# Early up blocks of a decoder block on one core: the second product is added to the first one's copy at once, and the row factors keep the order of the source

## The chip, the cores and the metric

One Trainium2 chip, one core. The metric is device time in microseconds (us), the median of several executions; lower is better. The profile is of one execution on the same core. Engines: TensorE (PE in the profile) for matmuls, VectorE (DVE), ScalarE (ACT), GpSimd (POOL), and the queue of SyncE (SP), which issues most transfers.

## The reference, cut to what matters

A decoder block: an RWKV-7 mixer beside sliding-window attention, both merged by gates, and then a gated feed-forward with a short convolution. All of it is float32, 512 rows, model width 2048, feed-forward width 5632. The change lies at the seam between the output projection and the feed-forward:

```python
x = x + (g_rw * p_rw + g_att * p_att) @ w_out[l]
x = x + conv_ffn(rms_norm(x, norm2_g[l]), w_up[l], conv_w[l], conv_b[l], w_down[l])

def conv_ffn(h, w_up, conv_w, conv_b, w_down):
    u = h @ w_up
    up = jnp.pad(u, ((0, 0), (CONV_W - 1, 0), (0, 0)))
    c = up[:, 0:S] * conv_w[0] + up[:, 1:S + 1] * conv_w[1] + up[:, 2:S + 2] * conv_w[2] + conv_b
    val, gate = jnp.split(c, 2, axis=-1)
    return (jax.nn.silu(gate) * val) @ w_down
```

## The kernel before, in words

Every large product runs in three matmuls of a reduced float32 form: each operand is split into a high part and a low part, and high·high, high·low and low·high are summed in PSUM. ScalarE makes the high part by a copy (`whi`, L1090, or L1055 for a row factor) and VectorE the low part by a subtraction (`wlo`, L1091, or L1056).

The three projections `w_out`, `w_up` and `w_down` are each done as 2x2 blocks with seven products instead of eight. For `w_up` the rows of the normalised input `h` are split into two halves and its 2048 channels into two halves; that gives four quarters: `q11`, `q12`, `q21`, `q22` (in the lists of instructions the tiles `x_13090`, `x_13091`, `x_13092`, `x_13093`). From them come seven **row factors**, each split into high and low once: `b11`, `b21`, `b22` are quarters themselves, and `t3 = q22 - q12`, `t1 = q11 - q12`, `t2 = -t1 - q22`, `t4 = -t2 - q21` are made in place in the quarters (tiles 128x2048). In the lists the pairs high/low are `t_15898`/`t_15899` for t1, `t_15900`/`t_15901` for t3, `t_15902`/`t_15903` for t2, `t_15904`/`t_15905` for t4 and `b_15896`/`b_15897` for b22.

The 5632 feed-forward columns go by in 44 **blocks** `f` of 128, value and gate together. Each block has seven **steps** P1, P2, P7, P6, P5, Q4, P3, each of 24 matmuls 128x256 (eight slices of channels by three matmuls). P1 and P2 are summed, the others go into a chain of sums. P1, P6, P5 and P3 of a block all write the same half of a PSUM bank (`X`), one after the other, so each waits until the one before has been taken out by ScalarE (L1124). In blocks 0 to 3 the sum of P2 goes to the other half of that same bank (`Z`).

A table `steps` sets the order: P1 of blocks 0 to 3, then P2 of blocks 0 to 3, then P7 of blocks 0 to 3; from there, for blocks 0 and 1, P6(0), P5(0), P6(1), P3(0), P5(1), Q4(0), P3(1), Q4(1), the same for blocks 2 and 3, and from block 4 on one block at a time. The first four blocks thus start on factors that exist early, while the rest of the row factors are being made. `run(i)` prepares step i+2 (`prep`: for P6 and P3 a sum of two weight tiles on VectorE, L1084, then `whi` and `wlo`), issues the matmuls of step i, and takes its result out (`Block.out`). From step 12 on, `prep` also issues up to two pieces of the convolution of earlier blocks. `whi` and `wlo` live in rings of three buffers, so the `whi` of a step waits for the matmuls of the step three before it.

The quarters `q12` and `q22` reach TensorE last: `transposed` multiplies them by a diagonal of the norm factors into PSUM (eight tiles of 128x256 in `ps_t`, L1039), and each is evicted with a scale, the even ones on ScalarE (L1048), the odd ones on VectorE (L1046).

Instructions of an engine run in the order in which they stand in its list. `pin` (`tc.keep_in_program_order`) keeps an instruction in the order of the source among all those that carry it; one without it is placed by a scheduler. In the kernel before, the evictions, the four passes that make t3, t1, t2, t4 and the splits of the row factors carry none.

In blocks 0 to 3, P1 is copied by ScalarE to a tile `t1` of its own (L1117, not the row factor), and the sum of P2 stays in PSUM until the tiles `u` of the convolution exist; then VectorE writes `u = t1 + Z` (L1128). This is done for blocks 0 and 1 ahead of step 12, P6(0), for block 2 behind P6(2), and for block 3 behind Q4(2).

Of the kernel before, what the change touches and what calls it, by code (L numbers as in the profile page):

```python
# [8 lines left out]
F32 = mybir.dt.float32  # L9
# [3 lines left out]
AF = mybir.ActivationFunctionType  # L13
ALU = mybir.AluOpType
# [120 lines left out]
def block_kernel(ctx: ExitStack, tc: tile.TileContext, d: Dims, a: dict, out: bass.AP):  # L135
# [723 lines left out]
    TH = S // 2  # L859
# [170 lines left out]
    def transposed(tps, i, q, dg=None):  # L1030

        pss = []
        for k in range(KH):
            if k % 2 == 0:
                pss.append(tps.tile([P, 2, TH], F32, name="ps_t", tag="tp"))
            for t in range(NT // 2):
                dst, src = pss[-1][:, k % 2, t * P : (t + 1) * P], q[:, t, k * P : (k + 1) * P]
                if dg:
                    pe.matmul(dst, src, dg[t], start=True, stop=True)  # L1039
                else:  # L1040
                    pe.transpose(dst, src, ident)
        for k in range(KH):
            src, g = pss[k // 2][:, k % 2], col("n2g", i * KH + k)
            dst = q[:, 2 * k // KH, k % (KH // 2) * TH : (k % (KH // 2) + 1) * TH]
            if k % 2:
                dve.tensor_scalar(dst, src, g, None, op0=ALU.mult)  # L1046
            else:
                act.activation(dst, src, AF.Copy, scale=g)  # L1048

    def halves(t):  # L1050
        return t.rearrange("p (a k) s -> p a (k s)", a=2)

    def split_q(n, q):
        hi, lo = (halves(x) for x in bq[n])
        act.activation(hi, q, AF.Copy)  # L1055
        dve.tensor_tensor(lo, q, hi.bitcast(F32), op=ALU.subtract)  # L1056

    us = []
    dve.tensor_scalar(cw[:, 0:3, NF:], cw[:, 0:3, NF:], -1.0, None, op0=ALU.mult)
# [4 lines left out]
    class Block:  # L1064
# [46 lines left out]
        def out(self, n):  # L1111
            X, Y, Z = self.X, getattr(self, "Y", None), self.Z
            if n == "P7":
                return
            if n == "P1" and self.f < NPRE:
                self.t1 = up.tile([P, TH], F32, name="t1", tag="t1", bufs=NPRE)
                pin(act.activation(self.t1, X, AF.Copy))  # L1117
                return

            i, j, ps, first = {"P1": (0, 0, X, True), "P2": (0, 0, Z, False), "P6": (1, 0, X, True), "P5": (1, 1, X, True),  # L1120
                               "Q4": (1, 0, Y, False), "P3": (0, 1, X, True)}[n]
            u = us[self.f % 2][:, i, 2 + j * TH : 2 + (j + 1) * TH]
            if first:
                pin(act.activation(u, ps, AF.Copy))  # L1124
                if n == "P5":
                    pin(dve.tensor_tensor(u, u, Y, op=ALU.add))
            else:
                pin(dve.tensor_tensor(u, self.t1 if n == "P2" and self.f < NPRE else u, ps, op=ALU.add))  # L1128

        def conv(self, part):  # L1130

# [75 lines left out]
    def run(i):  # L1207
        f, n = steps[i]
        prep(i + 2, 2 if 3 * NPRE <= i < 7 * NPRE else 1)
        B[f].mm(n)  # L1210
        if n != "P2" or f >= NPRE:
            B[f].out(n)
        if n == "P3":
            if f % 2 == 0:
                wp["add"] = sums_along()
# [45 lines left out]
    run(2)  # L1261
    transposed(tps, 0, q12, dg)
    run(3)
    dve.tensor_tensor(q11, q11, q12, op=ALU.subtract)
    transposed(tps, 1, q22, dg)
    tpx.close()
    run(4)
    dve.tensor_tensor(q12, q22, q12, op=ALU.subtract)
    split_q("t3", q12)
    tcx.close()  # L1270
    x1q.close()
# [3 lines left out]
    run(7)  # L1275
    upy = psx.enter_context(tc.tile_pool(name="uppy", bufs=4, space=PSUM, side="right", reuse_waits="tile"))
    run(8)
    dve.scalar_tensor_tensor(q11, q11, -1.0, q22, op0=ALU.mult, op1=ALU.subtract)
    split_q("t2", q11)
    run(9)  # L1280
    run(10)
    split_q("b22", q22)
    run(11)
    dve.scalar_tensor_tensor(q21, q11, -1.0, q21, op0=ALU.mult, op1=ALU.subtract)
    split_q("t4", q21)
    x1s.close()
    upu = upx.enter_context(tc.tile_pool(name="upu", bufs=1, side="left", reuse_waits="tile"))
# [5 lines left out]
    upc = upcx.enter_context(tc.tile_pool(name="upc", bufs=1, side="right", reuse_waits="tile"))  # L1293
    hp0 = upcx.enter_context(tc.tile_pool(name="hhl0", bufs=1, side="right", reuse_waits="tile"))
    for f in range(2):
        B[f].out("P2")
    for i in range(3 * NPRE, len(steps)):
        run(i)
        if steps[i] in ((2, "P6"), (2, "Q4")):
            B[2 + (steps[i][1] == "Q4")].out("P2")  # L1300
        if steps[i] == (NF - 2, "P7"):
            first_h = fetch("dn", 0, 0, hp0, pin)
        if steps[i] == (NF - 1, "P7"):
# [103 lines left out]
```

## Time and profile before

| | |
|---|---|
| device time, median of 3 runs | 2952.3 us (2951.39 to 2952.68) |
| profiled execution, first to last instruction | 2946.4 us |
| that span and the median differ by | 5.9 us |
| TensorE busy | 2897.7 us |
| VectorE busy | 1949.0 us |
| ScalarE busy | 1316.0 us |

The profiled execution gives the span, not the device time; the 5.9 us lie around the span. Times below are counted from the start of the span. "Idle before" is the time an engine stood still ahead of an instruction, with what ended it.

### The profile page before, as it was taken

To read this page: it belongs to the slowest core of one execution; us is meant where nothing else is said; L and a number is where in the kernel's file an instruction comes from. 1 tells how busy PE (TensorE), PEld (TensorE's weight loads), DVE (VectorE), ACT (ScalarE), POOL (GpSimd) and SP (SyncE) were. 2 spreads that over 40 slices of the span, in tenths; PEclk is the share of its full clock that TensorE was granted. 3 is DMA by queue.
4 is the path that set the end of the run, shared out by engine and by line. 5 is a ranking of instruction groups with operands and counts; after the bars stand their busy time and mean duration, and the time that the engine had idled before them with its cause. 6 is when DMAs were issued, how large, how long until landed. Compare 5 with 4: busy or idle time off the path is not lost.

```text
span 2946.4 us, 48467 instructions
## 1 busy us (share of the span) xinstructions
PE 2897.7 (98%) x18922; PEld 2473.2 (84%) x18922; DVE 1949.0 (66%) x3242; ACT 1316.0 (45%) x2134; POOL 219.4 (7%) x286
## 2 busy tenths in 40 slices
PE   7999999999999999999999899999999999999999
PEld 6777777777777777688888899999999999888887
DVE  5555666666666666344567877778777778665555
ACT  4344434434334334232346554554554555544444
POOL 0001000000000000101000011011011011000000
PEclk9999999999999999999999999999999999999999
DMA  6855656656656656878877788888888888877775
GB/s 185 210 151 153 178 139 154 159 129 161 158 131 162 155 129 170 250 223 262 275 243 247 193 242 236 230 227 225 234 239 235 227 229 237 311 240 242 256 258 189
DMA packets 225142, 609.47 MB, mean 207 GB/s; under 512 B 24768, under 2 KB 44944, under 8 KB 223888
## 3 DMA queue, kind: packets, MB, share of 16 engines
q1 hardware_dynamic: 157504, 434.92, 45.9%
q0 software_dynamic: 36064, 132.14, 23.3%
q10 hardware_dynamic: 31344, 39.31, 3.9%
q8 instruction: 148, 2.42, 0.3%
q14 instruction: 82, 0.67, 0.1%
HBM read 556.62 MB, written 174.43 MB: 248 GB/s over the span
## 4 chain that ended last, share of the span: by engine, by line
PE 92%; DVE 3%; ACT 2%; DMA 2%; issue 1%; ACTq 0%; SPq 0%; DVEq 0%
PE X L1108 17%; PE X L975 11%; PE acc L262 10%; PE acc L261 10%; PE acc L260 10%; PE Y L975 8%; PE Y L1108 8%; PE Z L1108 4%; PE psG L758 1%; PE bulk L689 1%; PE mi L505 1%; PE bulk L751 1%; PE psS L769 1%; PE bulk L728 1%; DMA raw<-in_w_z_dram 1%
## 5 line engine op out<-in xcount | busy, mean ns | idle before, releaser
L262 PE MATMUL acc<-xhi,wlo 128*128 128x512 f32 x1120 | 460.0, 411 | 0.7 <-DVE wlo L244 0.7
L260 PE MATMUL acc<-xhi,whi 128*128 128x512 f32 x1120 | 454.9, 406 | 4.0 <-ACT whi L243 4.0
L261 PE MATMUL acc<-xlo,whi 128*128 128x512 f32 x1120 | 453.9, 405 | 0.0
L243 ACT ACTIVATE whi<-raw 128x512 fp32r<-128x512 f32 x352 | 220.0, 629 | 491.3 <-PE acc L261 326.2
L968 DVE TENSOR_TENSOR wlo<-raw,whi 128x1024 fp32r<-128x1024 f32 x210 | 257.0, 1224 | 203.4 <-ACT whi L967 202.4
L244 DVE TENSOR_TENSOR wlo<-raw,whi 128x512 fp32r<-128x512 f32 x352 | 240.3, 688 | 205.1 <-ACT whi L243 198.1
L967 ACT ACTIVATE whi<-raw 128x1024 fp32r<-128x1024 f32 x210 | 222.6, 1060 | 289.3 <-PE X L975 151.8
L1108 PE MATMUL X<-b,whi 128*128 128x256 f32 x1472 | 270.4, 284 | 2.3 <-DVE u L1128 0.9
L1108 PE MATMUL X<-t,whi 128*128 128x256 f32 x1408 | 258.9, 284 | 8.7 <-DVE u L1128 8.3
L1091 DVE TENSOR_TENSOR wlo<-raw,whi 128x1024 fp32r<-128x1024 f32 x176 | 215.1, 1223 | 77.5 <-ACT whi L1090 77.2
L1108 PE MATMUL Y<-t,whi 128*128 128x256 f32 x1408 | 257.1, 283 | 0.0
L262 PEld LDWEIGHTS acc<-xhi,wlo 128*128 128x128 f32 x1120 | 211.3, 189 | 44.2 <-issue 3.1
L260 PEld LDWEIGHTS acc<-xhi,whi 128*128 128x128 f32 x1120 | 211.6, 189 | 43.2 <-ACT whi L243 5.2
L261 PEld LDWEIGHTS acc<-xlo,whi 128*128 128x128 f32 x1120 | 211.3, 189 | 40.3 <-issue 3.1
L1090 ACT ACTIVATE whi<-a 128x1024 fp32r<-128x1024 f32 x132 | 139.3, 1056 | 216.4 <-DVE a L1084 213.2
L1108 PEld LDWEIGHTS X<-b,whi 128*128 128x128 f32 x1472 | 230.7, 193 | 3.1 <-issue 2.4
L1108 PEld LDWEIGHTS X<-t,whi 128*128 128x128 f32 x1408 | 220.8, 193 | 9.3 <-DVE u L1128 5.7
L1108 PEld LDWEIGHTS Y<-t,whi 128*128 128x128 f32 x1408 | 219.6, 192 | 0.0
L1108 PE MATMUL X<-b,wlo 128*128 128x256 f32 x736 | 209.1, 284 | 2.1 <-DVE wlo L1091 2.1
L1091 DVE TENSOR_TENSOR wlo<-a,whi 128x1024 fp32r<-128x1024 f32 x132 | 161.7, 1226 | 68.2 <-ACT whi L1090 67.6
L1108 PE MATMUL X<-t,wlo 128*128 128x256 f32 x704 | 200.1, 284 | 0.1
L1108 PE MATMUL Y<-t,wlo 128*128 128x256 f32 x704 | 199.2, 283 | 0.0
(346 smaller groups left out, 6151.2 us busy)
## 6 DMA issues: line engine op xcount, KB each, us to landing
raw<-in_w_up_dram SPq DMA_DIRECT2D x180, 512.0 KB
raw<-in_w_z_dram SPq DMA_DIRECT2D x288, 256.0 KB
s_dn<-in_w_dn_dram POOLq DMA_DIRECT2D x88, 512.0 KB, 6.3
raw<-in_w_up_dram POOLq DMA_DIRECT2D x88, 512.0 KB, 8.7
raw<-s_dn SPq DMA_DIRECT2D x88, 512.0 KB
raw<-in_w_dn_dram SPq DMA_DIRECT2D x66, 512.0 KB
a<-in_w_up_dram SPq DMA_DIRECT2D x48, 512.0 KB
s_dn<-in_w_dn_dram SPq DMA_DIRECT2D x44, 512.0 KB
```

The source lines that it names most:

```text
L243: pin(act.activation(hi, raw, AF.Copy))
L244: pin(dve.tensor_tensor(lo, raw, hi.bitcast(F32), op=ALU.subtract))
L260: pe.matmul(acc, whi[:, j], xhi[:, k], start=first, stop=False)
L261: pe.matmul(acc, whi[:, j], xlo[:, k], start=False, stop=False)
L262: pe.matmul(acc, wlo[:, j], xhi[:, k], start=False, stop=last)
L505: pe.matmul(ps[:, h], pT[:, kb, h], vt[:, n - 1 + kb, g * HD : (g + 1) * HD], start=kb == kbs[0], stop=kb == kbs[-1])
L967: act.activation(whi, wr, AF.Copy)
L968: dve.tensor_tensor(wlo, wr, whi.bitcast(F32), op=ALU.subtract)
L975: pe.matmul(dst, l[:, q, ts], r[:, es], start=fst and j == 0, stop=lst and j == 2, skip_group_check=True)
L1090: pin(act.activation(hi, t, AF.Copy))
L1091: pin(dve.tensor_tensor(lo, t, hi.bitcast(F32), op=ALU.subtract))
L1108: pin(pe.matmul(ps, l[:, k], r[:, k], start=start and k + i == 0, stop=last and i == 2, skip_group_check=True))
```

## The change

It has four parts. The sum of P2 of blocks 0 to 3 is added to the copy `t1` as soon as P2 is done (VectorE, in place), and ScalarE copies `t1` to `u` where VectorE added before (`begin`). The evictions, the four passes and the splits of the row factors are pinned. In the two batches that use the diagonal, six of eight evictions go to ScalarE and two to VectorE, instead of four and four. And two lines of the source change places: the split of t2 stands behind `run(9)`, the pass that makes t1 behind the second batch.

```diff
-            if k % 2:
-                dve.tensor_scalar(dst, src, g, None, op0=ALU.mult)
+            if k % (4 if dg else 2) == 1:
+                pin(dve.tensor_scalar(dst, src, g, None, op0=ALU.mult))
             else:
-                act.activation(dst, src, AF.Copy, scale=g)
+                pin(act.activation(dst, src, AF.Copy, scale=g))
...
-        act.activation(hi, q, AF.Copy)
-        dve.tensor_tensor(lo, q, hi.bitcast(F32), op=ALU.subtract)
+        pin(act.activation(hi, q, AF.Copy))
+        pin(dve.tensor_tensor(lo, q, hi.bitcast(F32), op=ALU.subtract))
...
+            if n == "P2" and self.f < NPRE:
+                pin(dve.tensor_tensor(self.t1, self.t1, Z, op=ALU.add))
+                return
...
+        def begin(self):
+            pin(act.activation(us[self.f % 2][:, 0, 2 : 2 + TH], self.t1, AF.Copy))
...
     run(3)
-    dve.tensor_tensor(q11, q11, q12, op=ALU.subtract)
     transposed(tps, 1, q22, dg)
     tpx.close()
+    pin(dve.tensor_tensor(q11, q11, q12, op=ALU.subtract))
     run(4)
-    dve.tensor_tensor(q12, q22, q12, op=ALU.subtract)
+    pin(dve.tensor_tensor(q12, q22, q12, op=ALU.subtract))
...
-    dve.scalar_tensor_tensor(q11, q11, -1.0, q22, op0=ALU.mult, op1=ALU.subtract)
+    pin(dve.scalar_tensor_tensor(q11, q11, -1.0, q22, op0=ALU.mult, op1=ALU.subtract))
+    run(9)
     split_q("t2", q11)
-    run(9)
...
-    dve.scalar_tensor_tensor(q21, q11, -1.0, q21, op0=ALU.mult, op1=ALU.subtract)
+    pin(dve.scalar_tensor_tensor(q21, q11, -1.0, q21, op0=ALU.mult, op1=ALU.subtract))
...
     for f in range(2):
-        B[f].out("P2")
+        B[f].begin()
...
         if steps[i] in ((2, "P6"), (2, "Q4")):
-            B[2 + (steps[i][1] == "Q4")].out("P2")
+            B[2 + (steps[i][1] == "Q4")].begin()
```

Since the change moves instructions, three places of the order follow. First VectorE around the two batches of the diagonal, from the `wlo` of P2(0) on; before:

```order
L1091 TENSOR_TENSOR wlo<-raw,whi 128x1024
L1046 TENSOR_SCALAR x_13091<-ps_t,par 128x256 x4
L1264 TENSOR_TENSOR x_13090<-x_13090,x_13091 128x2048
L1091 TENSOR_TENSOR wlo<-raw,whi 128x1024
L1056 TENSOR_TENSOR t_15899<-x_13090,t_15898 128x2048
L1046 TENSOR_SCALAR x_13093<-ps_t,par 128x256 x4
L1091 TENSOR_TENSOR wlo<-raw,whi 128x1024
L1268 TENSOR_TENSOR x_13091<-x_13093,x_13091 128x2048
L1278 SCALAR_TENSOR_TENSOR x_13090<-x_13090,x_13093 128x2048
L1056 TENSOR_TENSOR t_15901<-x_13091,t_15900 128x2048
```

and now, from the evictions of the second batch on (L1116 is the new addition, on the tiles `t1` of blocks 0 to 3):

```order
L1046 TENSOR_SCALAR x_13093<-ps_t,par 128x256 x2
L1271 TENSOR_TENSOR x_13090<-x_13090,x_13091 128x2048
L1091 TENSOR_TENSOR wlo<-raw,whi 128x1024
L1116 TENSOR_TENSOR t_15941<-t_15941,X 128x256
L1273 TENSOR_TENSOR x_13091<-x_13093,x_13091 128x2048
L1056 TENSOR_TENSOR t_15901<-x_13091,t_15900 128x2048
L1091 TENSOR_TENSOR wlo<-raw,whi 128x1024
L1116 TENSOR_TENSOR t_15994<-t_15994,X 128x256
L1091 TENSOR_TENSOR wlo<-raw,whi 128x1024
L1116 TENSOR_TENSOR t_16028<-t_16028,X 128x256
L1056 TENSOR_TENSOR t_15899<-x_13090,t_15898 128x2048
L1091 TENSOR_TENSOR wlo<-raw,whi 128x1024
```

The pass for t1 (L1264, now L1271) and its low part have moved behind the second batch, the low part of t3 now comes ahead of that of t1, and the pass for t2 (L1278) has left this place. Second, VectorE up to the weight sum of P6(1); before (`a` tiles are weight sums, L1084: `a_16065` for block 0, then `a_16196`, now named `a_16198`, for block 1):

```order
L1084 TENSOR_TENSOR a_16065<-a_16065,raw 128x1024
L1284 SCALAR_TENSOR_TENSOR x_13092<-x_13090,x_13092 128x2048
L1091 TENSOR_TENSOR wlo<-a_16065,whi 128x1024
L1091 TENSOR_TENSOR wlo<-raw,whi 128x1024
L1056 TENSOR_TENSOR t_15905<-x_13092,t_15904 128x2048
L1128 TENSOR_TENSOR u_16391<-t_15941,X 128x256
L1128 TENSOR_TENSOR u_16393<-t_15994,X 128x256
L1084 TENSOR_TENSOR a_16196<-a_16196,raw 128x1024
```

and now:

```order
L1283 SCALAR_TENSOR_TENSOR x_13090<-x_13090,x_13093 128x2048
L1091 TENSOR_TENSOR wlo<-raw,whi 128x1024
L1056 TENSOR_TENSOR t_15903<-x_13090,t_15902 128x2048
L1084 TENSOR_TENSOR a_16065<-a_16065,raw 128x1024
L1091 TENSOR_TENSOR wlo<-a_16065,whi 128x1024
L1056 TENSOR_TENSOR b_15897<-x_13093,b_15896 128x2048
L1091 TENSOR_TENSOR wlo<-raw,whi 128x1024
L1289 SCALAR_TENSOR_TENSOR x_13092<-x_13090,x_13092 128x2048
L1056 TENSOR_TENSOR t_15905<-x_13092,t_15904 128x2048
L1084 TENSOR_TENSOR a_16198<-a_16198,raw 128x1024
```

The pass for t2 (L1283) and the low parts of t2 and b22, which stood further up before, now stand between the weights of P7(2) and the weight sum of P6(1), and the two additions to `u` are gone. Third, ScalarE at the same place; before:

```order
L1055 ACTIVATE t_15902<-x_13090 128x2048
L1090 ACTIVATE whi<-raw 128x1024 x2
L1090 ACTIVATE whi<-a_16065 128x1024
L1090 ACTIVATE whi<-raw 128x1024
L1055 ACTIVATE t_15904<-x_13092 128x2048
L1090 ACTIVATE whi<-a_16196 128x1024
L1124 ACTIVATE u_16391<-X 128x256
```

and now:

```order
L1055 ACTIVATE t_15902<-x_13090 128x2048
L1090 ACTIVATE whi<-a_16065 128x1024
L1055 ACTIVATE b_15896<-x_13093 128x2048
L1090 ACTIVATE whi<-raw 128x1024
L1055 ACTIVATE t_15904<-x_13092 128x2048
L1134 ACTIVATE u_16395<-t_15941 128x256
L1134 ACTIVATE u_16397<-t_15994 128x256
L1090 ACTIVATE whi<-a_16198 128x1024
L1127 ACTIVATE u_16395<-X 128x256
```

The high part of t2 now comes behind the `whi` of P7(2) and P7(3), that of b22 (before further up) behind the `whi` of P6(0), and the copies `begin` (L1134) stand ahead of the `whi` of P6(1). The last row, here L1127, before L1124, is in both lists the instruction that takes P6(0) out of `X`. The lists of TensorE, GpSimd and of the SP queue keep their order.

More of the change, by code (lines that the diff above doesn't have):

```diff
@@ L1127, in out @@
             else:
-                pin(dve.tensor_tensor(u, self.t1 if n == "P2" and self.f < NPRE else u, ps, op=ALU.add))
+                pin(dve.tensor_tensor(u, u, ps, op=ALU.add))
+        def begin(self):
+            pin(act.activation(us[self.f % 2][:, 0, 2 : 2 + TH], self.t1, AF.Copy))
         def conv(self, part):
@@ L1210, in run @@
         B[f].mm(n)
-        if n != "P2" or f >= NPRE:
-            B[f].out(n)
+        B[f].out(n)
         if n == "P3":
```

## The prediction

> **What bounds the kernel now.** I read the page first, then busy time by stage, then what TensorE waited for in the stage of the change, then the places of those waits.
>
> ```profile
> span 2946.4 us, 48467 instructions
> PE 2897.7 (98%) x18922; PEld 2473.2 (84%) x18922; DVE 1949.0 (66%) x3242; ACT 1316.0 (45%) x2134; POOL 219.4 (7%) x286
> ```
>
> TensorE is busy for 98% of the span. A change that leaves its work alone can only move the remaining idle time, or the clock. The stretches (TensorE busy, then weight loads, VectorE, ScalarE, GpSimd, granted clock, transfers) say where it lies:
>
> ```profile
> 1610.00:1715.04 105.04, 92.42 (x738) 91.28 (x739) 83.38 (x101) 56.41 (x75) 10.49 (x14) 0.95 0.80 222
> 1715.04:2521.00 805.96, 805.82 (x6713) 805.41 (x6713) 636.50 (x764) 413.66 (x562) 83.88 (x97) 1.00 0.86 231
> 2521.00:2946.40 425.40, 420.37 (x1857) 347.49 (x1856) 254.33 (x267) 202.14 (x231) 2.14 (x4) 1.00 0.74 251
> ```
>
> From 1715 us on TensorE hardly stops (0.14 us idle in 806), so a shift at 1715 reaches the end undiminished. Before it, in the first four blocks, 12.6 us are idle and the clock averages 0.95. There, by what ended each wait (us in total, times, longest):
>
> ```profile
> PE X L1108 <- DVE u L1128: 9.2, 3, 5.5
> PE X L1108 <- DVE wlo L1091: 2.1, 1, 2.1
> PE X L1108 <- DVE x L989: 0.9, 1, 0.9
> PE X L1108 <- ACT u L1124: 0.5, 1, 0.5
> PE X L1108 <- ACT whi L1090: 0.5, 1, 0.5
> ```
>
> Most of it is L1128, the late addition that the change takes away. The places, with the last matmul batch of the diagonal (start, length, instruction, idle before):
>
> ```profile
> 1625.49 3.73 PE L1039 MATMUL ps_t<-dg,x 128*128 128x128 f32 x32
> 1638.32 0.51 PE L1108 MATMUL X<-b,whi 128*128 128x256 f32 x2 [0.47 <-ACT whi L1090]
> 1640.97 0.58 PE L1108 MATMUL X<-b,wlo 128*128 128x256 f32 x1 [2.14 <-DVE wlo L1091]
> 1659.57 0.48 PE L1108 MATMUL X<-t,whi 128*128 128x256 f32 x2 [2.76 <-DVE u L1128]
> 1663.14 0.50 PE L1108 MATMUL X<-t,whi 128*128 128x256 f32 x2 [0.47 <-ACT u L1124]
> 1691.94 0.80 PE L1108 MATMUL X<-t,whi 128*128 128x256 f32 x2 [5.51 <-DVE u L1128]
> 1709.06 0.48 PE L1108 MATMUL X<-b,whi 128*128 128x256 f32 x2 [0.94 <-DVE u L1128]
> ```
>
> By the table of steps these are P2(3) (two rows), P6(0), P5(0), P5(2) and P3(3). A wait has an after-effect on the clock (column behind the count, windows chosen around the waits), and with it on the steps that follow (start, length, matmuls):
>
> ```profile
> 1641.00:1644.40 3.40, 3.40 (x16) 0.52 0.90 265
> 1692.00:1695.40 3.40, 3.40 (x16) 0.50 1.03 181
> 1695.40:1705.00 9.60, 9.60 (x82) 1.00 0.82 240
> 1656.80:1659.60 2.80, 0.04 (x2) 1.00 0.66 184
> ```
>
> ```profile
> 1663.14 11.77 PE X L1108 x96
> 1691.94 13.31 PE X L1108 x96
> 1712.16 2.88 PE Y L1108 x24
> ```
>
> A step takes 2.88 us, so 96 matmuls take 11.52. Behind the wait of 5.51 they took 13.31: 3.4 us at half clock, 1.79 us lost. Behind the waits at P6(0) and P5(0) the clock stayed at 1.00, and 0.25 us was lost.
>
> **The change, part by part.** What the removed addition frees is bounded by what is late next. Durations of the other pieces (mean ns behind the bar's busy time), then single rows of both engines around P6(0), P5(0) and P5(2):
>
> ```profile
> L1091 DVE TENSOR_TENSOR wlo<-raw,whi 128x1024 fp32r<-128x1024 f32 x16 | 19.4, 1222 | 4.1 <-ACT whi L1090 4.1
> L1090 ACT ACTIVATE whi<-raw 128x1024 fp32r<-128x1024 f32 x16 | 16.6, 1050 | 5.8 <-PE X L1108 3.2 <-PE Y L1108 2.5
> L1084 DVE TENSOR_TENSOR a<-a,raw 128x1024 f32<-128x1024 f32 x8 | 9.7, 1219 | 0.0
> L1056 DVE TENSOR_TENSOR t<-x,t 128x2048 fp32r<-128x2048 f32 x4 | 9.2, 2290 | 1.2 <-ACT t L1055 1.2
> L1055 ACT ACTIVATE t<-x 128x2048 fp32r<-128x2048 f32 x4 | 7.6, 1908 | 1.6 <-DVE x L1268 1.4
> L1048 ACT ACTIVATE x<-ps_t,par 128x256 f32<-128x256 f32 x8 | 3.5, 470 | 2.0 <-PE ps_t L1039 1.6 <-ACT x L1048 0.3
> ```
>
> ```profile
> 1649.65 1.22 DVE L1091 TENSOR_TENSOR wlo<-raw,whi 128x1024 fp32r<-128x1024 f32 x1
> 1650.79 1.22 DVE L1084 TENSOR_TENSOR a<-a,raw 128x1024 f32<-128x1024 f32 x1
> 1651.92 2.28 DVE L1284 SCALAR_TENSOR_TENSOR x<-x,x 128x2048 f32<-128x2048 f32 x1
> 1656.80 2.29 DVE L1056 TENSOR_TENSOR t<-x,t 128x2048 fp32r<-128x2048 f32 x1 [0.32 <-ACT t L1055]
> 1659.67 1.22 DVE L1084 TENSOR_TENSOR a<-a,raw 128x1024 f32<-128x1024 f32 x1
> 1691.47 0.41 DVE L1128 TENSOR_TENSOR u<-t,X 128x256 f32<-128x256 f32 x1
> 1661.01 1.06 ACT L1090 ACTIVATE whi<-a 128x1024 fp32r<-128x1024 f32 x1 [4.24 <-DVE a L1084]
> 1662.70 0.38 ACT L1124 ACTIVATE u<-X 128x256 f32<-128x256 f32 x1 [0.64 <-PE X L1108]
> 1690.24 0.36 ACT L1124 ACTIVATE u<-X 128x256 f32<-128x256 f32 x1
> ```
>
> The last row but one is the copy that lets P5(0) start. On ScalarE it stands behind the `whi` of P6(1), this waits for the weight sum of P6(1) on VectorE (1659.67), and that stands behind the low part of t4 (1656.80). The change keeps this queue, and pins the passes and splits of t2, b22 and t4 into it, where before VectorE had done t2 and b22 early. Consecutive rows of VectorE start 0.08 us before the one ahead ends (1649.65, 1650.79, 1651.92), so on one engine I take 1.14 for 128x1024, 2.21 for 128x2048, 0.34 for a small addition, 0.97 for `whi`; from engine to engine the full length plus 0.04.
>
> How far the start of the chain is pushed: the second batch ends on TensorE at 1629.2, the last two evictions on ScalarE (0.47 each) at 1630.1, the `whi` of P2(2) at 1631.1, its `wlo` at 1632.3. Then come one addition and the pass for t3, to 1634.9, its high part to 1636.8, its low part to 1639.1, and the `wlo` of P2(3) to 1640.3. P2(3) thus still waits, to 1640.35 instead of 1640.97. VectorE then has three additions, the `wlo` of P7(0), P7(1) and P7(2) and the low part of t1: 3x0.34 + 3x1.14 + 2.21 = 6.65, so the pass for t2 starts at 1646.9. From there the two engines alternate, each waiting for the other:
>
> | piece | ends (us) |
> |---|---|
> | pass for t2, VectorE | 1649.2 |
> | t2 high, ScalarE 1.91 | 1651.1 |
> | t2 low, VectorE (2.21 to the next) | 1653.4 |
> | weight sum P6(0), 1.22 | 1654.6 |
> | `whi` P6(0) (0.97 to the next) | 1655.6 |
> | b22 high, 1.91 | 1657.6 |
> | b22 low, then `wlo` P5(0): 2.21 + 1.14 | 1660.9 |
> | pass for t4, 2.29 | 1663.2 |
> | t4 high, then low: 1.91 + 2.21 | 1667.4 |
> | weight sum P6(1), 1.22 | 1668.6 |
> | `whi` P6(1) (0.97 to the next) | 1669.6 |
> | copy of P6(0) out of `X`, 0.38 | 1670.0 |
>
> P6(0) no longer waits for L1128 and runs from about 1655.7, with a short wait for its `wlo`, to 1659.6. Then TensorE stands still for 10.5 us, until P5(0) at 1670.1; before, it was 1663.14: **+7.0 us**.
>
> Behind that the clock will be at half: +1.79 as after the 5.51 wait, less the 0.25 lost there now: **+1.55**. Bounds: nothing if it behaves as behind 2.76, twice 1.79 if two such stretches pass; the long wait is nearest to 5.51.
>
> From P5(0) to P5(2) both lists agree, except for the copies `begin` on ScalarE. P5(2) waits for the addition (1691.47 + 0.41) and also for its own copy, done at 1690.60. Only the difference can go: **-1.3**; 4.2 of the 5.51 stay, with the half clock behind them (bounds: all of its 1.79 stays, or none). At P3(3) the 0.94 go: **-0.9**; its other operands are not reported as waited for.
>
> Edits without a term: the new additions (4x0.34 on VectorE) replace four of L1128, and both stand inside the table above. Four evictions move from VectorE to ScalarE at about the same price; ScalarE has room, but VectorE waits there for `whi`, inside the 1631.1 above. Transfers keep their order on all queues. A weight tile is free once its `wlo` is done; the one freed later than before, that of P7(1) at about 1645.5 by the sum above, is next used by the weight sum of P6(1) at 1667.4. Its two transfers of 512 KB would take some 5 us at the 222 GB/s of the stage's row (last column), so they stay hidden.
>
> Sum: 7.0 + 1.55 - 1.3 - 0.9 = +6.3. The profiled span would go from 2946.4 to 2952.7; the median of the runs shown, 2952.3, stands 5.9 above the profiled span, so the median becomes **2958.6 us**, slower by 0.21%.
>
> One rule weighed: the wait at P2(3), 0.47 + 2.14 with two matmuls between, was followed by 3.4 us at 0.52. The Trainium skill (TensorE: Matmul & The Clock Gate, section "Part 1: The HAM clock gate") has the half clock come after at least one idle window of about 3.4 us. By its words the present wait would be too short and the trace differs; taken so for the changed kernel, P2(3) would end 1.7 us earlier. VectorE holds the chain back there, so the pass for t2 would still start at 1646.9 and the sum would be the same 6.3; by the row P2(3) ends near 1644.7, the `whi` of P7(2) follows it, and the pass starts 0.2 later, 6.5.
>
> **The rivals.**
> - *The bank wait was the bound, and the row factors stay hidden* (the other side). For it: 9.2 us of waits carry L1128's name. Then P6(0) starts 2.7 earlier and P5(0) follows at once; with 1.3 and 0.9 gained and the half clock at P5(2) gone (1.79), -6.7: 2945.6. It decides at the copy of P6(0): done by 1663.1 in the changed kernel, no loss at that place. Against it: the table needs 23 us from the pass for t2, in pieces that depend on each other.
> - *The stall comes, the clock costs nothing net*: half clock behind P5(0), but not behind the shortened wait at P5(2): 6.3 - 1.8 = +4.5, or neither, +3: about 2956. For it: 2.76 left the clock at 1.00, and 4.2 lies between 2.76 and 5.51.
> - *A longer half clock*: two stretches behind 10.5 us: +8.1, 2960.4. For it: the wait is twice the longest seen.
> - *The change does not free the bank*: then P6(0) would still wait for L1116 or `begin`. The additions are queued before 1646.9, so nothing comes of it; only the gain at P5(2) and P3(3) could fail, +8.5, 2960.8.
>
> **How the numbers follow.** Sum as worked out 0.45 (2957.8 to 2959.5 alone, with 0.05 us of hand-over in each of 14 pieces); clock free 0.28; longer clock or bank not freed 0.19; rival on the other side 0.08. About 0.2%, 5.9 us, is what a measurement of this kernel can tell from no change: the limit is 2958.2, just under the sum, so four fifths of the first case and all of the third are slower, 0.55; the clock-free case and the rest 0.38 the same; 0.07 faster. The range leaves out the other side and the far ends: 2954.3 to 2961.3, from +2.0 (both clocks free, hand-overs shorter by 0.7) to +9.
>
> **What would show it.** Right: no wait on an addition into `u` or `t1` anywhere; one wait of about 10 us ahead of P5(0), ended by ScalarE's copy out of `X`, behind the `whi` of P6(1); a wait of about 4.2 ahead of P5(2), ended by ScalarE; the stretch from the first step to P1(4) longer by about 6. VectorE idle for some 2 us each ahead of the low parts of t3 and t4. Wrong: a copy of P6(0) done before 1666, or the low part of t4 done before 1663, would take the stall away, and with it the sign.

## The result: slower by 0.31%

| | before | changed |
|---|---|---|
| device time, median | 2952.7 us (2951.4 to 2957.6, 7 runs) | 2964.2 us (2959.2 to 2966.0, 7 runs) |
| ratio of the times, 95% interval | | 1.0031 (1.0021 to 1.0042) |
| profiled execution, span | 2946.4 us | 2963.6 us |

The ratio is 9 us (6 to 12) of slowdown; the two medians differ by 11.5. 2958.6 was predicted, with 2961.3 as the upper end. The sign was right, the size was not.

First the stretch from the first up step, P1(0), to P2(4), behind which both kernels run alike (TensorE is busy for 799.20 and 799.16 of the next 800 us). Time, TensorE busy, weight loads, VectorE, ScalarE, GpSimd, granted clock, DMA share, GB/s; before:

```profile
1610.34:1723.68 113.34, 101.06 (x810) 99.89 (x811) 90.65 (x108) 59.63 (x80) 11.02 (x15) 0.95 0.81 220
```

The changed kernel:

```profile
1614.96:1740.35 125.39, 105.73 (x810) 104.31 (x811) 89.61 (x104) 62.37 (x88) 11.34 (x15) 0.89 0.75 200
```

The start differs by 4.62 us although the code ahead of it is the same: profiles of 15 further kernels, one of them the kernel before again, put that first step between 1610.15 and 1618.56. So only lengths are compared from here on. The stretch is 12.05 us longer: 4.67 more busy for the same 810 matmuls (the clock), 7.38 more idle. What TensorE waited for in it (total, times, longest):

```profile
PE X L1108 <- ACT u L1127: 15.3, 2, 10.2
PE X L1108 <- DVE wlo L1091: 2.8, 3, 2.0
PE X L1108 <- ACT whi L1090: 1.4, 1, 1.4
PE X L1108 <- DVE x L989: 0.8, 1, 0.8
```

The additions no longer stand there; in their place is ScalarE's copy out of `X`, with 15.3 us where L1128 had 9.2. Its places, and the rest of the waits:

```profile
1643.89 0.50 PE L1108 MATMUL X<-b,whi 128*128 128x256 f32 x2 [1.42 <-ACT whi L1090]
1646.41 0.58 PE L1108 MATMUL X<-b,wlo 128*128 128x256 f32 x1 [2.02 <-DVE wlo L1091]
...
1663.71 0.38 PE L1108 MATMUL X<-t,wlo 128*128 128x256 f32 x1 [0.29 <-DVE wlo L1091]
1676.77 0.80 PE L1108 MATMUL X<-t,whi 128*128 128x256 f32 x2 [10.16 <-ACT u L1127]
...
1707.73 0.79 PE L1108 MATMUL X<-t,whi 128*128 128x256 f32 x2 [5.15 <-ACT u L1127]
...
1737.44 0.39 PE L1108 MATMUL X<-t,wlo 128*128 128x256 f32 x1 [0.49 <-DVE wlo L1091]
```

These are P2(3) (two rows), P6(0), P5(0), P5(2) and P6(4). The 10.16 ahead of P5(0) is the stall that was predicted. The chain that leads to it and to the next one (start, length, what; in order of time):

```profile
1646.41 5.06 PE X L1108 x22
...
1654.60 1.23 DVE x L1283
1655.85 1.93 ACT t L1055
...
1660.01 1.23 DVE a L1084
...
1662.31 1.91 ACT b L1055
...
1666.45 1.22 DVE wlo L1091
1667.67 2.21 DVE x L1289
1669.90 1.92 ACT t L1055
...
1674.06 1.23 DVE a L1084
...
1675.39 1.06 ACT whi L1090
1676.45 0.28 ACT u L1127
...
1676.77 8.56 PE X L1108 x48
...
1687.96 4.62 DMA raw<-in_w_up_dram
...
1693.14 11.15 DMA raw<-in_w_up_dram
...
1704.31 1.24 DVE a L1084
...
1707.41 0.28 ACT u L1127
...
1707.73 14.19 PE X L1108 x96
```

Up to the copy at 1676.45 it is the table of the prediction piece by piece: pass for t2, t2 high, weight sum of P6(0), b22 high, `wlo` of P5(0), pass for t4, t4 high, weight sum of P6(1), its `whi`, the copy. Behind P5(0) a transfer joins it: the accumulating part of a weight tile of block 3 took 11.15 us to land, and VectorE's sum for P6(3) waited for it.

### The profile page after: what moved, and what is told of

Its sections match the earlier page's. It is cut to its first block, busy times and chain, and to the rows that moved or that the text cites. A ratio compares the mean times of both kernels' runs of the same rounds, so it can differ in the third digit from the quotient of the medians.

```text
span 2963.6 us, 48467 instructions
## 1 busy us (share of the span) xinstructions
PE 2904.8 (98%) x18922; PEld 2477.7 (84%) x18922; DVE 1948.3 (66%) x3238; ACT 1318.7 (44%) x2142; POOL 219.1 (7%) x286
## 4 chain that ended last, share of the span: by engine, by line
PE 90%; DMA 3%; DVE 3%; ACT 2%; issue 1%; ACTq 0%; SPq 0%; POOL 0%; DVEq 0%; POOLq 0%
PE X L1108 17%; PE X L975 11%; PE acc L262 10%; PE acc L261 10%; PE acc L260 10%; PE Y L975 8%; PE Y L1108 8%; PE Z L1108 4%; DMA raw<-in_w_z_dram 1%; PE psG L758 1%; PE mi L505 1%; PE bulk L751 1%; PE psS L769 1%; PE bulk L689 1%; PE bulk L728 1%
## 5 line engine op out<-in xcount | busy, mean ns | idle before, releaser
L1108 PE MATMUL X<-t,whi 128*128 128x256 f32 x1408 | 262.3, 287 | 15.4 <-ACT u L1127 15.3
```

The lines of the kernel that those rows point to most:

```text
L1108: pin(pe.matmul(ps, l[:, k], r[:, k], start=start and k + i == 0, stop=last and i == 2, skip_group_check=True))
```

## The experiments

All times are counted from the first up step of the same profile. "P2(4)" is the length of the whole stretch. The medians of the kernel before beside these runs lay at 2953.5 to 2954.8 us. Each length comes from a single execution, and executions of one kernel differ: the profiled ones of the rows "the same, P6(0) copied first", "the same, P6(2) too", "other order, all pinned" and "before, fewer transfers" took 3.8, 3.4, 3.9 and 8.1 us more than the medians of their kernels, those of the other kernels with a ratio of their own at most 1.9 more or less. So the ratio says whether a kernel is faster, and the lengths say where its time goes; a difference of a microsecond or two between two lengths alone proves little. The experiments ran on four chips, each beside the kernel before on the same chip.

| kernel | wait ahead of P5(0) | P5(0) | P5(2) | P2(4) | ratio to before (95%) |
|---|---|---|---|---|---|
| before, first profile | 0.47 | 52.80 | 81.60 | 113.34 | 1 |
| before, second profile | 0.47 | 55.36 | 84.66 | 116.18 | |
| changed | 10.16 | 61.81 | 92.77 | 125.39 | 1.0031 (1.0021 to 1.0042) |
| early addition alone | 5.63 | 55.37 | 84.79 | 117.10 | 1.0007 (0.9998 to 1.0016) |
| changed, addition late | 0.47 (11.71 at P6(0)) | 63.99 | 93.39 | 125.04 | 1.0030 (1.0019 to 1.0042) |
| changed, evictions 4 and 4 | 10.17 | 61.20 | 91.11 | 123.72 | 1.0028 (1.0017 to 1.0040) |
| changed, passes and splits unpinned | 5.64 | 56.20 | 86.56 | 118.81 | 1.0010 (1.0001 to 1.0019) |
| changed, t4 behind step 13 | 3.69 | 54.75 | 89.57 | 121.55 | 1.0023 (1.0014 to 1.0033) |
| changed, P6(0) copied first | 6.14 | 57.13 | 89.87 | 121.86 | 1.0032 (1.0019 to 1.0045) |
| early addition, t4 pass early | 3.02 | 54.13 | 83.46 | 115.60 | 1.0000 (0.9991 to 1.0009) |
| the same, P6(0) copied first | 0.47 | 51.57 | 82.49 | 115.04 | 0.9995 (0.9986 to 1.0004) |
| the same, P6(2) too | 0.47 | 50.49 | 75.38 | 112.80 | 0.9994 (0.9985 to 1.0002) |
| the same, fewer transfers | 0.47 | 51.74 | 76.62 | 112.21 | 0.9983 (0.9974 to 0.9991) |
| other order, all pinned | 0.47 | 48.13 | 79.89 | 117.29 | 1.0002 (0.9993 to 1.0011) |
| other order, fewer transfers | 0.47 | 48.12 | 79.31 | 116.18 | 1.0003 (0.9995 to 1.0012) |
| changed, fewer transfers | 10.17 | 61.22 | 90.90 | 123.71 | 1.0026 (1.0015 to 1.0037) |
| before, fewer transfers | 0.47 | 55.23 | 84.10 | 116.67 | 0.9995 (0.9986 to 1.0004) |

**Which part costs.** The early addition by itself (the kernel before with `begin` and the addition of P2 at once), the changed kernel without it, the changed kernel with evictions as before, and the changed kernel without the pins on passes and splits.

```diff
 # early addition alone: before, and
+            if n == "P2" and self.f < NPRE:
+                pin(dve.tensor_tensor(self.t1, self.t1, Z, op=ALU.add))
+                return
...
 # changed, addition late: the same lines taken out again
...
 # changed, evictions 4 and 4
-            if k % (4 if dg else 2) == 1:
+            if k % 2:
...
 # changed, passes and splits unpinned
-    pin(dve.tensor_tensor(q12, q22, q12, op=ALU.subtract))
+    dve.tensor_tensor(q12, q22, q12, op=ALU.subtract)
...
```

> The kernel before with the early addition of P2 and the copies into u alone; passes, splits and evictions without pins, evictions 4 and 4. Theory A (the fixed order of the row factors is the whole cost, the early addition a gain): the pass for t2 again starts within 1 us of the pass for t3, no wait on an addition ahead of P6(0) and P5(2), P5(0) starts 0 to 2 us earlier than before, and the time is 2 to 6 us under before. Rival B (the early addition itself costs: four additions on VectorE ahead of the row factors, two copies ahead of the copy out of X): P5(0) starts at least 3 us later and the time is 3 us or more over before. Rival C (no effect): within 1 us of before, the waits only renamed.

> The changed kernel with its additions of P2 put back to the late place (u = t1 + Z on VectorE, no copies into u); pins, source order and 6-and-2 evictions stay. Theory A: the wait of about 10 us ahead of P5(0) stays (9 to 12), the waits on the additions at P6(0), P5(2), P3(3) come back in part, and the time is 10 to 16 us over before, not less than the changed kernel. Rival B: the wait ahead of P5(0) falls under 6 us and the time is within 6 us of before.

> The changed kernel with four evictions of each diagonal batch on VectorE and four on ScalarE, as before; everything else stays. Theory A with its reading of the trace (ScalarE's six evictions stand in a row, and VectorE's wait for ScalarE's of the same tile, which holds the passes for t1 and t3): the last eviction ends 1 to 2 us earlier, P2(3) waits 1 to 2 us less, the wait ahead of P5(0) is 1 to 2 us shorter, and the time is 1 to 3 us under the changed kernel. Rival D (moving four evictions costs nothing, as predicted): within 0.5 us of the changed kernel in the wait ahead of P5(0).

> The changed kernel without the pins on the four passes and the splits; early addition, 6-and-2 evictions and the moved source lines stay. Theory A (the fixed order of passes and splits is the cost): the pass for t2 goes back beside the pass for t3, the wait ahead of P5(0) is 5 to 6 us as in the first experiment, the stretch from the first step to P2(4) 116 to 119 us, the time 6 to 9 us under the changed kernel and 0 to 4 over before. Rival D2 (the six evictions on ScalarE are what counts): the stretch stays over 122 us and the time within 3 us of the changed kernel.

Without the early addition the stretch is as long as with it (125.04 against 125.39): the chain now holds L1128, and the stall stands one step earlier. The time is the changed kernel's too, 9 us over before, where I had expected 10 to 16.

```profile
1671.03 0.77 PE L1108 MATMUL X<-t,whi 128*128 128x256 f32 x2 [11.71 <-DVE u L1128]
```

Without the pins on passes and splits it shrinks by 6.58 us, to a length within the expected 116 to 119, and the time falls by about 6 us, with intervals that do not meet. So the fixed order of the row factors is the larger part of the cost: shown. The evictions, against what I had said, do not matter: the wait ahead of P5(0) did not change (10.17), and the time cannot be told from the changed kernel's. P5(0) came 0.61 earlier, but it did so as well in the changed kernel with fewer transfers (61.22), whose evictions are 6 and 2: these 0.6 us belong to the profiled execution of the changed kernel (see below).

The early addition alone missed the 2 to 6 us that I had expected to gain: the interval allows from 0.6 gained to 4.7 lost. Its trace shows why. P6(0) no longer waited, and P5(0) waited 5.63 instead, since without pins the scheduler now put the pass for t4 behind the `wlo` of P5(0) (VectorE):

```profile
1658.01 1.23 DVE L1091 TENSOR_TENSOR wlo<-raw,whi 128x1024 fp32r<-128x1024 f32 x1
1659.15 2.29 DVE L1289 SCALAR_TENSOR_TENSOR x<-x,x 128x2048 f32<-128x2048 f32 x1
1663.41 2.29 DVE L1056 TENSOR_TENSOR t<-x,t 128x2048 fp32r<-128x2048 f32 x1 [1.98 <-ACT t L1055]
1665.62 1.22 DVE L1084 TENSOR_TENSOR a<-a,raw 128x1024 f32<-128x1024 f32 x1
```

In the kernel before, the pass ran at 1651.92, 41.58 us after the first step; here at 46.18.

**Which piece of the chain.** In the changed kernel, t4 made later; and P6(0) copied out of `X` before P6(1) is prepared.

```diff
 # t4 behind step 13 (x1s.close() and the pool behind it move along)
     run(11)
-    pin(dve.scalar_tensor_tensor(q21, q11, -1.0, q21, ...))
-    split_q("t4", q21)
...
+    run(3 * NPRE)
+    run(3 * NPRE + 1)
+    pin(dve.scalar_tensor_tensor(q21, q11, -1.0, q21, ...))
+    split_q("t4", q21)
...
 # P6(0) copied first
-        prep(i + 2, ...)
+        if i != 3 * NPRE: prep(i + 2, ...)
         B[f].mm(n)
         B[f].out(n)
+        if i == 3 * NPRE: prep(i + 2, 2)
```

> The changed kernel with the pass and the split of t4 put behind step 13, P5(0), instead of ahead of step 12, P6(0); t4 is used first in step 17. Theory A (the copy of P6(0) is late because the serial chain of VectorE and ScalarE stands ahead of it): the pass, the high and the low part (2.21 + 1.91 + 2.21 = 6.3 us) leave the chain, the wait ahead of P5(0) falls from 10.2 to about 4, the half clock behind it shrinks with it, and the time is 5 to 9 us under the changed kernel, unless t4 comes late for step 17 (then less). Rival E (the transfer for block 3 is what counts, since it lands when it does whatever the order): the wait ahead of P5(2) grows by what the other loses, and the time is within 2 us of the changed kernel.

> The changed kernel, pins and all, with the exchange in step 12 alone (P6(0) taken out ahead of the preparation of P6(1)). Theory A: the copy of P6(0) follows the two copies into u, about 3.9 us earlier than in the changed kernel; the wait ahead of P5(0) falls from 10.2 to about 6.3, one of 2 to 3.5 us appears ahead of P6(1), whose weights come as late as before, and the time is 1 to 4 us under the changed kernel. Rival (it is P6(1)'s weights that bound the stage, wherever the wait lies): the two waits add up to the 10.2 less one step of 2.9 and what the half clock gives back; under 1 us gained if the half clock covers both.

The t4 pieces left the chain as worked out (wait 3.69, "about 4"), and P5(0) came 7.06 us earlier, nearly back at the kernel before; but of that only 3.84 us reached P2(4). P5(2) now waited 5.73, and a new wait of 1.75 for a `wlo` came at 1683.07, behind the t4 pieces, which VectorE now did there. Copying P6(0) first moved P5(0) by 4.68, and the wait ahead of P5(2) grew from 5.15 to 6.82; the wait of 2 to 3.5 us that I had expected ahead of P6(1) did not come. P2(4) came 3.53 earlier in the trace, but the times do not tell this kernel from the changed one. In both, part of what P5(0) gained was lost again at P5(2).

**What the early addition is worth once its followers are moved.** The early addition alone, with the pass for t4 pinned ahead of step 10; then P6(0) copied first, too; then also P6(2), in step 20.

```diff
+    pin(dve.scalar_tensor_tensor(q21, q11, -1.0, q21, ...))
     run(10)
...
-        if i != 3 * NPRE: prep(i + 2, ...)
+        if i not in (3 * NPRE, 5 * NPRE): prep(i + 2, ...)
```

> The early addition alone (as in the first experiment), and the pass for t4 pinned ahead of step 10, so that it stands ahead of the weight sum of P6(0) on VectorE; in the first experiment it came 46.2 us after the first up step, in the kernel before 41.6. Theory A2 (the early addition gains at P6(0), and the late pass for t4 ate that): the pass at 40 to 41 us after the first step, P5(0) about 2.2 us earlier than in the first experiment (53.1 after the first step, before 52.8), the half clock behind it mostly gone, the time 2 to 4 us under the first experiment and within 2 us of before. Rival B2 (the early addition is worth nothing because of what it adds on VectorE): the same time as the first experiment within 1 us.

> As the one before, and in step 12 the result of P6(0) is taken out ahead of the preparation of P6(1), so that the copy out of X no longer stands behind the high part of P6(1) on ScalarE. Theory A (a queue on ScalarE holds the copy, not the work of P6(0)): P5(0) starts within 0.6 us of the end of P6(0), about 50.4 us after the first step, no wait of more than 1 us ahead of P5(0), at most 2 us ahead of P6(1); 2 to 5 us under the kernel before if P5(2) moves along. Rival E (transfers set P5(2) whatever comes earlier): P5(0) early, but the wait ahead of P5(2) is longer by as much, and the time stays within 1 us of before.

> As the one before, and the same exchange in step 20: P6(2) is taken out ahead of the preparation of P6(3). Theory A: the wait of 4 to 6 us ahead of P5(2) goes; what stays of it lies ahead of P6(3), one step of 2.9 us later, and ends on the weights of P6(3) (transfer, sum, high part, low part); the time is 2 to 4 us under the kernel with the exchange at P6(0) alone, and 5 to 9 us under before. Rival E: the wait only moves to P6(3) in its full length: less than 1 us gained.

Each step shortened the wait that it aimed at (5.63 to 3.02, to 0.47; then 6.55 ahead of P5(2) to 0.53), and the stretch went 117.10, 115.60, 115.04, 112.80. In times, none of the three can be told from the kernel before, so the 2 to 5 and 5 to 9 us that I had expected to gain with the copies did not show; all three are faster than the changed one, whose interval lies wholly above theirs. P6(0) first alone gained 2.56 at P5(0) and gave 1.59 back at P5(2), whose wait grew from 4.69 to 6.55; only with P6(2) moved as well did P5(2) come earlier, by 7.1, and seven waits of 0.46 to 1.35 us behind it, 4.95 in sum, took back most of that.

**The kernel before, a second time.**

> The kernel before, unchanged, for a second profile. If its first profile is typical, the first up step starts near 1610.3 and the stretch from there to P2(4) takes 113.3 us again. The other profiles so far, whose code ahead of that step is the same, started it at 1611.2 to 1615.4; so I expect a start in that span, and a stretch of 113 to 116 us: longer than 113.3 if the clock behind the waits of 2.8 and 0.5 us at P6(0) and P5(0) also falls to half in some executions.

The start lies ahead of the expected span, and the stretch, 116.18, just above it. The same instructions, nearly the same waits, another clock. Second profile:

```profile
1640.77 0.58 PE L1108 MATMUL X<-b,wlo 128*128 128x256 f32 x1 [2.15 <-DVE wlo L1091]
1660.52 0.77 PE L1108 MATMUL X<-t,whi 128*128 128x256 f32 x2 [2.76 <-DVE u L1128]
1665.51 0.50 PE L1108 MATMUL X<-t,whi 128*128 128x256 f32 x2 [0.47 <-ACT u L1124]
```

and behind the wait of 2.76, the windows (TensorE busy and granted clock as above), first profile, then second:

```profile
1659.57:1662.50 2.93, 2.93 (x24) 2.89 (x24) 1.72 (x3) 1.06 (x1) 0.86 (x1) 1.00 0.14 20
```

```profile
1660.52:1663.50 2.98, 2.98 (x14) 2.98 (x15) 1.78 (x3) 1.06 (x1) 0.86 (x1) 0.50 0.31 22
```

In the chain the step that follows the wait, P6(0), reads, first profile, then second:

```profile
1659.57 3.11 PE X L1108 x24
```

```profile
1660.52 4.53 PE X L1108 x24
```

The whole stretch in the second profile:

```profile
1610.15:1726.33 116.18, 103.38 (x810) 102.22 (x811) 90.80 (x108) 59.71 (x80) 11.35 (x15) 0.93 0.81 216
```

It is 2.84 us longer than in the first profile, 2.32 of it in TensorE's busy time; the wait ahead of P5(2) grew by 0.5 (5.51 to 6.02). Against this second profile the changed kernel's stretch is 9.21 us longer, which agrees with the measured ratio (9 us); against the first it is 12.05, at the upper end of the ratio's interval.

**Pins in another order.** Everything pinned, as in the changed kernel, each piece placed by its first user, evictions 4 and 4, P6(0) and P6(2) copied first.

```diff
     run(3)
+    pin(dve.tensor_tensor(q11, q11, q12, op=ALU.subtract))
+    split_q("t1", q11)
     transposed(tps, 1, q22, dg)
...
     run(4)
     pin(dve.tensor_tensor(q12, q22, q12, op=ALU.subtract))
+    run(5)
     split_q("t3", q12)
...
```

> Everything pinned as in the changed kernel, early addition too, but in another order, each piece by its first user: pass and split of t1 ahead of the second batch; the weights of P2(3) ahead of the split of t3; the pass for t2 behind that split; the low part of b22 behind step 12, the pass for t4 behind step 13 and its split behind step 14; P6(0) and P6(2) taken out ahead of the next preparation; evictions 4 and 4. Theory A (not the pin but the order that it fixes costs): no wait over 3 us anywhere in the stage, P2(3) without its 2.6 us, P5(0) at 47 to 50 us after the first step, the stretch to P2(4) 107 to 112 us, the time 2 to 7 us under before. Rival F (pinning itself costs, whatever the order): over before by 3 us or more. Rival E (transfers bound the stage): waits ahead of steps of blocks 2 and 3 that end on a transfer, and a time within 2 us of before.

With this order P2(3) lost its wait but 0.36, and P5(0) came at 48.13, the earliest but for its twin with fewer transfers (48.12). So pins need not make P5(0) late, and rival F, 3 us or more over before, is nearly out (the interval ends at 3.2). But the stretch was 117.29, not the 107 to 112 of theory A, and the time that of before. After P5(0), ten of the next seventeen steps waited 0.2 to 1.9 us for `whi`, `wlo` or a copy, and the chain ran over two transfers:

```profile
1657.69 8.01 DMA raw<-in_w_up_dram
...
1665.72 1.24 DVE a L1084
...
1687.25 10.65 DMA raw<-in_w_up_dram
...
1697.92 1.24 DVE a L1084
```

This pinned order still costs something: with fewer transfers in both (below), the kernel with the early addition, t4's pass early and both copies first is at 0.9983 of before and the other order at 1.0003, with intervals that do not meet. Whether any pinned order reaches what the scheduler finds is not shown.

**Transfers.** In four kernels the two sums of `w_down` slices that fall into blocks 0 to 3 (2 MB of the stretch's 25) are done in blocks 12, 13, 24 and 25.

```diff
-            if f % 2 == 0:
+            if f >= NPRE and f % 2 == 0:
                 wp["add"] = sums_along()
-            else:
+            elif f >= NPRE:
                 wp["add"]()
+        if n == "Q4" and f in (12, 24):
+            wp["add2"] = sums_along()
+        if n == "Q4" and f in (13, 25):
+            wp["add2"]()
```

> The changed kernel, with the two sums of w_down slices that fall into blocks 0 to 3 (two transfers of 512 KB each, one of them accumulating) done in blocks 12, 13 and 24, 25 instead. Theory A+E (the chain of VectorE and ScalarE sets P5(0), a transfer sets P5(2) in part): the wait ahead of P5(0) stays at 10 us, the accumulating transfer for P6(3) lands in 6 to 8 us instead of 11.2, the wait ahead of P5(2) falls from 5.2 to about 4.2, the time 1 to 3 us under the changed kernel. Rival (transfers play no part): the same waits as in the changed kernel within 0.3 us.

> The kernel before, with the same two sums done later. Theory A+E: P5(0) unchanged, P5(2) at most 1 us earlier, since in the kernel before no step of the stage was seen to wait for a transfer; within 2 us of before. If transfers bind the stage throughout, as its 25 MB at 220 GB/s would have it: 4 us or more under before.

> The kernel with the early addition, the early pass for t4 and P6(0) and P6(2) taken out first, with the same two sums done later. Theory E (transfers are what is late there next): the stretch from the first step to P2(4) falls from 112.8 to 106 to 110 us, and the time is 4 to 8 us under before. Rival (VectorE is the next bound, at 90 us busy of 113): 112 us and within 3 us of before.

> The kernel with everything pinned in the other order, with the same two sums done later. Theory E: its chain, which ran over two transfers for weight sums of 8.0 and 10.7 us, shortens; the stretch falls from 117.3 to 108 to 113 us and the time is 3 to 8 us under before. Rival: it stays over 115 us, VectorE's and ScalarE's queues being what is late.

In the changed kernel the transfer left the chain ahead of P5(2), and the wait fell to 4.22 us, what the prediction had given for it:

```profile
1703.07 0.80 PE L1108 MATMUL X<-t,whi 128*128 128x256 f32 x2 [4.22 <-ACT u L1127]
```

The stretch is 1.68 shorter, but the time cannot be told from the changed kernel's, and the kernel with evictions 4 and 4 and all its transfers has the same length (123.72) and a wait of 4.56 there. In the kernels with P6(0) and P6(2) copied first and with the other order it is shorter by 0.6 and 1.1 us, and in the kernel before 0.5 longer than in the second profile, 3.3 longer than in the first. So transfers are not the bound of the stage that its 25 MB at 220 GB/s made me suspect; the other order stayed over 115 us, as its rival said. What TensorE waited for in the kernel with both copies first and fewer transfers:

```profile
PE X L1108 <- DVE wlo L1091: 4.1, 5, 2.1
PE X L1108 <- ACT u L1127: 3.8, 4, 2.1
...
PE X L1108 <- ACT whi L1090: 0.8, 1, 0.8
PE Y L1108 <- DVE wlo L1091: 0.5, 1, 0.5
```

That kernel (early addition unpinned as before, t4's pass ahead of step 10, P6(0) and P6(2) copied first, two sums later) is faster than both, the kernel before and the changed one: 2949.1 us, 0.9983 of before. Its stretch, 112.21, is the one that the rival gave, its time the one of theory E. How much of it the later sums bring is not settled: its interval overlaps with that of the kernel without them (0.9985 to 1.0002), and the traces differ by 0.6 us.

## Why the prediction missed

The mechanism held, and three terms of the sum were too small: the start of the chain, the half clock, and the transfers, which had no term. By the prediction's own steps, in the first profile of before and that of the changed kernel:

| step | predicted | measured |
|---|---|---|
| P5(0) later | +7.0 | +9.01 |
| P5(0) to P5(2): half clock, less the gain at P5(2) | +1.55 - 1.3 | +2.16 |
| P5(2) to P2(4): the wait at P3(3) goes | -0.9 | +0.88 |
| sum | +6.3 | +12.05 |

- **The mechanism was right**: no wait on an addition; one wait of about 10 us ahead of P5(0) (10.5 predicted), behind the `whi` of P6(1); VectorE idle for 2 us ahead of the low parts of t3 and t4 (the two rows of VectorE below). From the pass for t2 to the end of the copy the trace takes 23.2 us (1653.53 to 1676.71), the table 23.1.

```profile
1642.92 2.29 DVE L1056 TENSOR_TENSOR t<-x,t 128x2048 fp32r<-128x2048 f32 x1 [2.04 <-ACT t L1055]
...
1671.85 2.29 DVE L1056 TENSOR_TENSOR t<-x,t 128x2048 fp32r<-128x2048 f32 x1 [1.98 <-ACT t L1055]
```

- **The start of the chain was mis-sized by 2.0 us.** The pass for t2 was to start at 1646.9, 36.6 after the first step; it started at 1653.53, 38.57. The step that failed is "the second batch ends ..., the last two evictions on ScalarE ... at 1630.1", with the `wlo` of P2(2) right behind its `whi`: the pass for t1 (2.2 us), which the change puts between them on VectorE, has no term. I let VectorE finish its two evictions early and do the pass under the `whi` of P2(2). In the changed kernel VectorE's last eviction stood behind one of ScalarE's:

```profile
1632.76 0.47 ACT L1048 ACTIVATE x<-ps_t,par 128x256 f32<-128x256 f32 x1 [1.09 <-PE ps_t L1039]
1633.65 1.57 ACT L1048 ACTIVATE x<-ps_t,par 128x256 f32<-128x256 f32 x4 [0.42 <-PE ps_t L1039]
```

```profile
1634.53 0.48 DVE L1046 TENSOR_SCALAR x<-ps_t,par 128x256 f32<-128x256 f32 x1 [2.12 <-ACT x L1048]
1634.93 2.28 DVE L1271 TENSOR_TENSOR x<-x,x 128x2048 f32<-128x2048 f32 x1
1637.13 1.22 DVE L1091 TENSOR_TENSOR wlo<-raw,whi 128x1024 fp32r<-128x1024 f32 x1
```

  The pass for t1 thus ended at 1637.2 and the `wlo` of P2(2) at 1638.35, 23.4 after the first step instead of 22.0. The two evictions read the two halves of one `ps_t` tile. The Trainium skill (PSUM — Partial Sum Buffer, "PSUM bank collisions raise a hardware error") says that two engines may not be on one bank's partitions at once and that the compiler's scheduler puts a dependency between them; the wait of 2.12 agrees with it. But this wait alone is not what made the pass late. With evictions 4 and 4 VectorE's last three waited for TensorE's batch instead,

```profile
1633.21 1.27 DVE L1046 TENSOR_SCALAR x<-ps_t,par 128x256 f32<-128x256 f32 x3 [1.30 <-PE ps_t L1039]
```

  and the pass for t1 started 19.94 us after the first step, against 19.97 in the changed kernel. The other 0.6 us lie behind P2(3): its last 22 matmuls took 5.06 us (4.33 before), and the `whi` of P7(2), ahead of the pass for t2 in the queues, waited for them; the prediction had allowed 0.2 for that. This was the clock of one execution, 0.50 behind that wait throughout (4.89 us), not the change: three kernels with the same instructions and waits up to there took 4.29 to 4.39, the one with fewer transfers for example

```profile
1643.61 4.39 PE X L1108 x22
```

- **The half clock behind the long wait** cost 2.80 (8.56 us for 48 matmuls that take 5.76), not 1.79 in this execution; the prediction's "two such stretches" was nearer. The clock stood at 0.50 for 3.43 us and at 0.66 in the 3.40 after that.
- **The gain at P5(2) did not come**: its wait is 5.15, not 4.2. The step "they stay hidden" failed. I looked at one weight tile, and at a mean rate; the one that was late is the tile for P6(3), whose accumulating transfer took 11.15 us. With fewer transfers it left the chain and the wait was 4.22: shown. How much of the 0.93 it makes is open, since with all transfers, and one of 10.16 in the chain, the kernel with evictions 4 and 4 waited 4.56.
- **The 0.9 at P3(3)** went as said, but the half clock took 14.19 us for the 96 matmuls behind P5(2) (13.31 before), and a wait of 0.49 came at P6(4).
- **The base was a short execution.** "The 5.9 us lie around the span" was wrong: in every run listed, before and changed, the time is 1.7 to 1.8 above its span. The first profile of before was thus an execution some 4 us under the median, 2.8 of it in this very stretch, mostly by the clock. Against the second profile, whose time of 2952.3 lies near the medians, the table would read +6.45, +1.66 and +1.10: P5(0) then falls under the prediction, and the misses are the transfer and the clock. Which of the two lengths is the typical one, two executions cannot say: the ratio of 9 us and the time of that execution speak for the second, while the 11.5 us between the medians lie nearer to the first. The kernel before with fewer transfers (55.23 at P5(0), 116.67 in all) does not decide it, as its profiled execution was the slowest of twelve.

Of the rivals, "the change does not free the bank" (2960.8) lies nearest by its number, but the change did free it; "a longer half clock" (2960.4) came true in part (2.80 of twice 1.79). The other side, that the bank wait was the bound, is refuted by the kernel with the early addition alone: what stood behind the addition was nearly as late. Even with t4's pass early again, P5(0) still waited 3.02, and the time was that of before.

## What to carry over

A wait that a trace puts on one instruction is worth only its distance to the next late thing in the queue: here 2.76 us of waiting for an addition hid a copy on ScalarE that stood behind another step's weights, and freeing the bank alone gained nothing that the times show. Pinning fixes what a scheduler had spread over idle places, so write down for each pinned piece its first user before choosing the order, and give every piece that moves a term on its engine: the pass for t1 had none. Of the two orders pinned here, neither was faster than the scheduler's own. Before working out a difference of 0.2%, take the same stretch from two profiles of the same kernel: here they differed by 2.8 us, and look where the time of each profiled execution lies among the times of its kernel.

## What the hardware did unexpectedly

After the same wait of 2.76 us the clock stayed at 1.00 in one execution and fell to 0.50 in another, with 1.4 us lost in that one step (24 matmuls in 4.53 us against 3.11). So a wait's length alone does not say whether the half clock follows. The Trainium skill (TensorE: Matmul & The Clock Gate, "Part 1: The HAM clock gate") has a free-running window and, for the start of a kernel, a number of cold matmuls that varies from run to run; these two profiles show the like in the middle of one. Its "after ≥1 idle window (~3.4µs)" does not fit a half clock behind 2.76 us, and the measurement decides. An accumulating transfer of 512 KB took 8.0, 10.7 and 11.2 us to land where it stood in the chain; the plain transfer of the same tile ahead of the last one took 4.62.
